# Hybrid attention encoder on one core: other homes for the second attention's first tiles, gates four deep, a fifth row buffer in the merge, another order of the first weights

## The chip, the core and the metric

The kernel runs on one NeuronCore of a Trainium2 chip. The metric is the device time of one execution in microseconds. The core's engines each work through their own instruction list in order: TensorE (PE: matmuls, and their weight loads as PEld), VectorE (DVE), ScalarE (ACT), GpSimd (POOL) and SyncE (SP), which here issues most DMAs; some are issued by ScalarE. An instruction waits for semaphores of others; what stands behind it on the same engine waits with it.

## The reference, cut to what matters

One layer of a bidirectional encoder over 2048 tokens of width 1024, all in float32:

```
h  = RMSNorm(x)
z  = h @ W_in  -> [q_A | k_A | v_A | q_B | k_B | v_B | gate_A | gate_B]
yA = windowed attention |t-s| <= 128, 8 heads, 2 groups of keys and values, ALiBi, a sink per head
yB = 2-D neighbourhood attention (8 heads, 32 rows x 64 columns, window 8 x 16) with a learned bias
x  = x + (sigmoid(gate_A) * (yA @ Wp_A) + sigmoid(gate_B) * (yB @ Wp_B)) @ W_out
x  = x + relu(RMSNorm(x) @ W_up)^2 @ W_down
out = RMSNorm(x)
```

## The kernel before, in words

Every float32 product is made of three matmuls on split operands: a high part (a cast to fp32r, by ScalarE) and a low part (the rest, by VectorE or GpSimd), so `mm3` (L200 to L203) issues high x high, high x low and low x high. Weights come as a slice of 128 columns in a tile `raw` (`load_slice`, L185 to L189; three buffers) and are split into `whl` (L176 to L178, two buffers): ScalarE casts (L177), GpSimd subtracts (L178).

The stages, in order:

1. The input projection of token blocks 0 and 1 in "quads" (matmuls at L252 to L254). Blocks 2 and 3 are only normalised and turned, and stored in DRAM (`h1d`).
2. The first attention (`attn_a`, from L667): 32 tiles (2 groups of 4 heads x 16 blocks of 128 queries). TensorE makes the scores (L680, L681; PSUM tag `s`, three banks); VectorE evicts them with bias and maximum (L682) into `sa`; ScalarE takes the exponent; GpSimd divides (L693). In a second step TensorE turns the probabilities (L699), they are split (`ph` L702, `pl` L703), TensorE multiplies them by the values (L704, L705, tag `av`, one bank), and the result goes by `ya` (L708, L709) to DRAM (`y_a`).
3. The second attention (`attn_b`, from L819): 32 units (8 heads `h`, each with four column blocks `j`). A unit loads queries `qb` (L824) and values `vb` (L827); per head `load_k` loads keys `kb0` or `kb1` (L814 to L816, 2.1 MB). Scores are L837, the eviction with bias L842 into `sb` (twelve buffers), the division L852 on GpSimd, the turning L864, the splits L869 and L870, the products L875; the result `yb` goes to `y_b`. `make_bias_b` adds the masks to a bias pattern `braw` on GpSimd (L805), into `biass` (j = 0 and 3, two buffers) or `biasl` (j = 1, kept for 2; one buffer).
4. The merge, four blocks of 512 tokens (from L1167). For each of eight features `f`, `gated(f, n)` (from L1174) multiplies weights by the pages of yA (n = 0) and yB (n = 1), 12 matmuls each; loads the stored gate `z` (L1183); takes its sigmoid (L1184, ScalarE); multiplies (L1185, VectorE). GpSimd adds both (L1197), ScalarE makes the high part `mh` (L1198), VectorE the low part `ml` (L1199). Then four rows of 128 tokens x two halves of 24 matmuls with W_out (PSUM `pt`, two banks), added to the row of x in `xr` by VectorE (L1217), normalised and turned (L1228). `load_y` (from L918) loads a block's yA and yB (`yraw`, L924) and splits them into pages (L930, L931).
5. The MLP: seven products for each quad (L252 to L254, `b`), up and down.

**Plain pieces.** What is left of the input projection, blocks 2 and 3, is cut into tiles of 24 matmuls (`qk_tile`, `v_tile`, `gate_tile`: L201 to L203 in PSUM tag `mm`) which `chain` (L714) yields in order, loading weights two tiles ahead and splitting them one ahead. `paced` (L736) sets each piece after the end of an attention unit: `at = n * 32 // total - lag`. In the first attention, 24 pieces; in the second, 44 with total = 40 and lag 4, of which pieces 20 to 43 are issued after `load_y(0)`. The pieces read the pages `hT` (blocks 2 and 3, L603 to L613), which are loaded (L609) and split ahead of everything else in stage 2.

**Who sets the order.** The program is written with waits (`issue_after`) and priorities by place; the order of each engine's list is then fixed when the program is built. It is the same in every execution.

**Homes.** On-chip memory is a stack from the left and one from the right. A new pool lies where an older one was closed, and a new tile waits until the tiles whose bytes it lies over are done. The first attention has, by the partition: on the right, from the end, `biasa0` (6 KB, bias of group 0), `va0` (8 KB), `ka0` (16 KB), `biasa1` (6 KB); on the left `ka1` (16), `va1` (8), `qa`, `sa`, `dist`, `ph`, `pl`, `ya`, `sta`. Group 0 is finished nine tiles before group 1. The second attention's pools of before, on the right: `masks` (12.5 KB), `braw` (2), `biass` (7.5), `biasl` (5), `kb0` (16), `qb` (6), `kb1` (16). So the masks lie over `biasa0` and `va0`; `braw`, `biass` and `biasl` over `va0` and `ka0`; `kb0` over the end of `ka0`, all of `biasa1` and free room; `qb` beyond it, where the left stack's last tiles (`ya`, `sta`) lie.

Of the kernel before, what the change touches and what calls it, by code (L numbers as in the profile page):

```python
# [8 lines left out]
F32 = mybir.dt.float32  # L9
# [6 lines left out]
D = 1024  # L16
# [6 lines left out]
P = 128  # L23
KC = D // P
NB = 4
BT = 512
# [66 lines left out]
def encoder_layer(ctx, tc, x, norm_mix, w_in, b_gate, sink, rpb, w_pa, w_pb, w_out,  # L93
# [12 lines left out]
    def pools(stack, side, tags, name):  # L106

        return {t: pool(f"{name}_{t}", side=side, stack=stack) for t in tags}
# [490 lines left out]
    ap_ = pools(s_a, "left", ("ka1", "va1", "qa", "sa", "dist", "ph", "pl", "ya", "sta"), "a")  # L599
    ap_.update(pools(s_a, "right", ("biasa0", "va0", "ka0", "biasa1"), "a"))  # L600
    hp = {}
    for b in (2, 3):
        hi, lo = [], []  # L603
        for p in range(2):
            h, l = (T(hpl[2 * (b - 2) + p], PAGE, F32R, "hT", 2) for _ in range(2))
            for n, (hh, ll) in enumerate(zip(halves(h), halves(l))):
                raw = T(wp, [P, KC, P], F32, "raw", 3).rearrange("p (k a) c -> p k (a c)", k=2)
                r = p * BT + n * 256
                SY.dma_start(raw, h1d[b - 2][r : r + 256, :].rearrange("(k p) t -> p k t", p=P))  # L609
                split(raw, hh, ll, V)  # L610
            hi.append(h)
            lo.append(l)
        hp[b] = hi, lo  # L613


    def qk_tile(col, scale, tiled=False):
# [96 lines left out]

    def chain(gens):  # L714

        for g in gens[:2]:
            next(g)
        next(gens[0])
        for k, g in enumerate(gens):
            if k + 2 < len(gens):  # L720
                next(gens[k + 2])
            if k + 1 < len(gens):
                next(gens[k + 1])
            yield from g
# [11 lines left out]
    def paced(filler, pieces, total, lag):  # L736

        for n in pieces:
            at = n * 32 // total - lag
            with tc.issue_after(done[at]) if at >= 0 else nullcontext():  # L740
                next(filler, None)

# [16 lines left out]
    for t in range(4):  # L759
        dense.append(qk_tile(O_KB + t * P, 0.125))  # L760
        dense.append(qk_tile(O_QB + t * P, 1.0, tiled=True))
        dense.append(v_tile(O_VB + t * P))
    fill = chain(dense + [gate_tile(f, (2, 3)) for f in range(16)])
    for g in (1, 0):
        make_bias_a(g)

# [13 lines left out]


    s_b = ExitStack()
    bp = pools(s_b, "right", ("masks", "braw", "biass", "biasl", "kb0", "qb", "kb1"), "b")
    bp.update(pools(s_b, "left", ("vb", "sb", "phb", "plb", "yb", "stb"), "b"))
    boff, bstart, btotal = bias_layout()
    masks = T(bp, [P, btotal], F32, "masks", 1)
    with tc.issue_after(began[20]):
# [28 lines left out]
        SY.dma_start(k[64:128, 1].bitcast(F32), kd[0:64])  # L816
        return k

    def attn_b(h, j, k, bias):  # L819
        e, t = h % 2, h // 2  # L820
        w, jt = B_W[j], JT[j]
        kp = 4 * w
        q = T(bp, [P, 4, P], F32R, "qb", 3)
        SY.dma_start(q.bitcast(F32), qs_b[t][e, :, j])  # L824
        yield
        v = T(bp, [P, 8, P], F32R, "vb", 3)
        SY.dma_start(v[: 4 * w].rearrange("p (b c) d -> p b (c d)", b=4).bitcast(F32),  # L827
                     vs_b[t][4 * B_C0[j] : 4 * (B_C0[j] + w), :, e * 256 : e * 256 + 256])
        st = T(bp, [P, 4, 4], F32, "stb", 6)
        mx, nm, sm, ri = (st[:, n, :] for n in range(4))  # L830
        kv = k.rearrange("p z (q f) -> p z q f", q=8)
        s = []
        for i in range(4):
            n = B_NR[i] * w
            ps = psum("s", 3)
            for z in range(2):
                PE.matmul(ps[:, :n], q[:, i, :],  # L837
                          kv[:, z, B_R0[i] // 4 : (B_R0[i] + B_NR[i]) // 4, 4 * B_C0[j] : 4 * (B_C0[j] + w)],
                          start=z == 0, stop=z == 1)
            o = boff[(jt, IT[i])]  # L840
            si = T(bp, [P, 512], F32, "sb", 12)
            V.tensor_tensor_reduce(out=si[:, :n], in0=ps[:, :n], in1=bias[:, o : o + n], scale=1.0, scalar=-3.0e38,  # L842
                                   op0=ALU.add, op1=ALU.max, accum_out=mx[:, i : i + 1])
            s.append(si)
        V.tensor_scalar(nm, mx, -0.125, None, ALU.mult)
        for i in range(4):
            n = B_NR[i] * w
            A.activation(s[i][:, :n], s[i][:, :n], AF.Exp, bias=nm[:, i : i + 1], scale=0.125, accum_out=sm[:, i : i + 1])
        V.reciprocal(ri, sm)
        for i in range(4):  # L850
            n = B_NR[i] * w
            G.tensor_scalar(s[i][:, :n], s[i][:, :n], ri[:, i : i + 1], 1.0, ALU.mult, ALU.mult)  # L852
        yield
        flush()
        po = psum("av", 1)
        first = True
        for pair in range(4):
            pt = psum("pt", 2)
            at, pieces = 0, []
            for c in (2 * pair, 2 * pair + 1):  # L860
                i0, ni = B_USE[c]
                for i in range(i0, i0 + ni):
                    rr = (4 * c - B_R0[i]) * w
                    PE.transpose(pt[:kp, at + (i - i0) * P : at + (i - i0 + 1) * P], s[i][:, rr : rr + kp], ident)  # L864
                pieces.append((c, i0, ni, at))
                at += ni * P
            ph = T(bp, [P, 512], F32R, "phb", 3)
            pl = T(bp, [P, 512], F32R, "plb", 3)
            A.copy(ph[:kp, :at], pt[:kp, :at])  # L869
            V.tensor_tensor(out=pl[:kp, :at], in0=pt[:kp, :at], in1=ph[:kp, :at].bitcast(F32), op=ALU.subtract)  # L870
            if pair == 0:
                pieces.reverse()
            for c, i0, ni, o in pieces:
                for z, src in enumerate((ph, pl)):
                    last = PE.matmul(po[:, i0 * P : (i0 + ni) * P], v[:kp, c, :],  # L875
                              src[:kp, o : o + ni * P], start=first, stop=(c == 7 and z == 1),
                              skip_group_check=True).ins
                    first = False
        done.append(last)

        y = T(bp, [64, BT], F32, "yb", 2)
        A.copy(y, po[64:128, :])
        V.tensor_tensor(out=y, in0=po[0:64, :], in1=y, op=ALU.add)
        put(y_b[t].rearrange("(e d) (i j t) -> e d i j t", e=2, i=4, j=4)[e, :, :, j, :],
            y.rearrange("d (i t) -> d i t", i=4))

    def all_b():
        for h in range(BH):
            k = load_k(h)
            for j in range(4):  # L890
                if j != 2:
                    bias = make_bias_b(h, JT[j])
                u = attn_b(h, j, k, bias)
                next(u)
                yield u

# [8 lines left out]

    units = ahead_of(all_b(), 1)
    drive((next(units) for _ in range(15)), live, False)
    paced(fill, range(20), 40, 4)
    flush()
    drive(units, live, True)  # L910
    flush()
# [23 lines left out]

    first_y = load_y(0)
    first_load = last_dma[0]
    paced(fill, range(20, 44), 40, 4)
    s_h.close()


# [6 lines left out]
    wo = []  # L948

    def load_wo(n):  # L950
        rv = T(p4x, [P, D], F32, "xr", 4)
        SY.dma_start(rv, w_out[0][n * P : (n + 1) * P, :])
        hl = T(pwo, [P, 2, D], F32R, "wo", 8)
        A.copy(hl[:, 0], rv)
        V.tensor_tensor(out=hl[:, 1], in0=rv, in1=hl[:, 0].bitcast(F32), op=ALU.subtract)
        wo.append(hl)
# [211 lines left out]
    for b in range(NB):  # L1168
        yh, yl = next_y
        mh = T(p4x, [P, KC, BT], F32R, "mh", 1)  # L1170
        ml = T(p4x, [P, KC, BT], F32R, "ml", 1)
        hls, gates = {}, {}

        def gated(f, n):  # L1174

            if n == 0:
                hls[f] = slice_of([(cols(w_pa[0], f * P), 4), (cols(w_pb[0], f * P), 4)])
            hl = hls[f]
            ps = psum("mm" if n == 0 else "s", 2 if n == 0 else 3)
            for c in range(4):  # L1180
                mm3(ps, hl[:, 0, 4 * n + c, :], hl[:, 1, 4 * n + c, :], yh[n][:, c], yl[n][:, c], c == 0, c == 3)
            g = T(wp, [P, 2, BT], F32, "z", 2)[:, 0] if n else T(p4, [P, BT], F32, "z", 4)
            SY.dma_start(g, zg[b][0][n, f * P : (f + 1) * P, :])  # L1183
            A.activation(g, g, AF.Sigmoid, bias=bg[:, 8 * n + f : 8 * n + f + 1])  # L1184
            V.tensor_tensor(out=g, in0=ps, in1=g, op=ALU.mult)  # L1185
            gates[f, n] = g
# [20 lines left out]
        tiles = []  # L1207
        for t in range(4):
            row0 = b * BT + t * P
            xt = load_tile(p4x, "xr", 4, xf[row0 : row0 + P])  # L1210
            for c in range(2):
                xc = xt[:, c * BT : (c + 1) * BT]
                ps = psum("pt", 2)
                for k in range(KC):
                    mm3(ps, mh[:, k, t * P : (t + 1) * P], ml[:, k, t * P : (t + 1) * P],
                        wo[k][:, 0, c * BT : (c + 1) * BT], wo[k][:, 1, c * BT : (c + 1) * BT], k == 0, k == KC - 1)
                V.tensor_tensor(out=xc, in0=ps, in1=xc, op=ALU.add)  # L1217
            flush()
            put(x2d[b][t * P : (t + 1) * P], xt)
            tiles.append(xt)  # L1220
# [227 lines left out]
```

## Time and profile before

| what | value |
| --- | --- |
| median of 3 runs | 2719.89 us (2717.86 to 2721.3) |
| the profiled execution's own time | 2720.12 us |
| its span, first to last instruction | 2718.3 us |
| mean granted TensorE clock | 0.990 |
| TensorE busy | 2637.6 us, 97% |
| stages, from the trace | first attention from 371.8 us, second from 689 us, merge from 1080 us, MLP from 1490 us |

How to read it: a line of a group or a timeline gives line number, engine, operation and tiles (out<-in). An idle time stands in brackets with the engine and line that ended it. In the rows of stretches the columns are the stretch, its length, then the busy time (and the number of instructions) of PE, PEld, DVE, ACT and POOL, the granted clock of TensorE, the share of DMA time and GB/s. A matmul's own length in the timeline (0.39 us) is more than the distance of two matmuls, since they are pipelined.

### The profile page before, as it was taken

The page shows a single profiled execution, that of the slowest core. Times are in us where ns is not written, and L with a number is a line of the kernel's source. Part 1 is how long each engine was busy: PE and PEld are TensorE (multiplying, and loading weights), DVE is VectorE, ACT ScalarE, POOL GpSimd, SP SyncE. Part 2 cuts the span into 40 slices and gives each one's busy share as a digit, 9 for nine tenths or more (in the row PEclk, how much of TensorE's full clock was granted, in tenths as well). Part 3 has the DMA queues.
Part 4 walks back from the last instruction along what each step waited for, and adds up shares of the span by engine and source line. Part 5 has one row for each costly group of instructions (what it writes and reads, how often), then busy time and mean ns, then how long its engine had stood idle before and what let it go on. Part 6 is the DMA issues. An engine that isn't in the chain of part 4 may idle for free.

```text
span 2718.3 us, 35079 instructions
## 1 busy us (share of the span) xinstructions
PE 2637.6 (97%) x12332; PEld 2184.2 (80%) x12332; DVE 1556.1 (57%) x2348; ACT 1251.4 (46%) x2229; POOL 843.8 (31%) x671
## 2 busy tenths in 40 slices
PE   7999999999899999898999999989999999999998
PEld 6888878777788888686787788878888888888887
DVE  7756466665454543633436667676664634545766
ACT  6334346665455555533533544554445333332444
POOL 1111233343555542531430456545553000000001
PEclk9999999999999999999999999999999999999999
DMA  4756385456777654734636556564435944445555
GB/s 148 200 155 196 135 240 149 109 142 162 210 198 189 184 152 141 260 121 151 229 109 225 190 200 209 178 208 163 144 129 190 335 155 159 149 149 178 174 191 169
DMA packets 329535, 480.86 MB, mean 177 GB/s; under 512 B 27896, under 2 KB 162168, under 8 KB 327184
## 3 DMA queue, kind: packets, MB, share of 16 engines
q1 hardware_dynamic: 300432, 445.06, 52.2%
q10 hardware_dynamic: 28928, 33.56, 3.9%
q8 instruction: 97, 1.59, 0.2%
q14 instruction: 78, 0.64, 0.1%
HBM read 323.28 MB, written 155.26 MB: 176 GB/s over the span
## 4 chain that ended last, share of the span: by engine, by line
PE 85%; DMA 6%; DVE 5%; ACT 2%; issue 1%; SPq 0%; POOL 0%; ACTq 0%; POOLq 0%; DVEq 0%
PE b L254 14%; PE b L252 14%; PE b L253 14%; PE mm L201 5%; PE mm L202 5%; PE mm L203 5%; PE zb L254 3%; PE zb L252 3%; PE zb L253 3%; PE av L875 2%; PE pt L201 2%; PE pt L202 2%; PE pt L203 2%; PE pt L864 2%; PE s L837 2%
## 5 line engine op out<-in xcount | busy, mean ns | idle before, releaser
L253 PE MATMUL b<-dwh,dah 128*128 128x512 f32 x896 | 348.5, 389 | 0.0
L254 PE MATMUL b<-dwh,dah 128*128 128x512 f32 x896 | 347.7, 389 | 0.0
L252 PE MATMUL b<-dwh,dah 128*128 128x512 f32 x896 | 338.1, 389 | 1.6 <-ACT dwh L248 1.6
L245 POOL TENSOR_TENSOR uc<-uc,uc 128x512 f32<-128x512 f32 x120 | 233.5, 1961 | 208.9 <-issue 136.3
L248 ACT CAST dah<-da 128x1024 fp32r<-128x1024 f32 (+1 forms) x128 | 121.0, 945 | 366.2 <-PE b L254 240.6
L249 DVE TENSOR_TENSOR dah<-da,dah 128x1024 fp32r<-128x1024 f32 (+1 forms) x128 | 139.3, 1090 | 224.4 <-ACT dah L248 219.6
L252 PE MATMUL b<-ubh,uwhlb 128*128 128x512 f32 x592 | 231.2, 391 | 3.3 <-DVE uc L245 2.2
L254 PE MATMUL b<-ubh,uwhlb 128*128 128x512 f32 x592 | 230.5, 391 | 3.2 <-DVE uwhlb L249 3.2
L253 PE MATMUL b<-ubh,uwhlb 128*128 128x512 f32 x592 | 230.9, 390 | 0.0
L201 PE MATMUL mm<-hT,whl 128*128 128x512 f32 x544 | 219.1, 403 | 4.5 <-ACT whl L177 2.3
L245 DVE TENSOR_TENSOR uc<-b,uc 128x512 f32<-128x512 f32 x160 | 108.8, 688 | 191.7 <-PE b L254 149.7
L203 PE MATMUL mm<-hT,whl 128*128 128x512 f32 x544 | 214.8, 395 | 0.0
L202 PE MATMUL mm<-hT,whl 128*128 128x512 f32 x544 | 214.5, 394 | 0.0
L178 POOL TENSOR_TENSOR whl<-raw,whl 128x1024 fp32r<-128x1024 f32 x66 | 160.2, 2428 | 148.8 <-ACT whl L177 142.4
L1338 POOL TENSOR_TENSOR st<-st,power 128x1 f32<-128x1 f32 x16 | 13.6, 857 | 613.8 <-DVE st L1337 613.6
L252 PEld LDWEIGHTS b<-dwh,dah 128*128 128x128 f32 x896 | 168.1, 188 | 36.9 <-ACT dwh L248 2.0
L254 PEld LDWEIGHTS b<-dwh,dah 128*128 128x128 f32 x896 | 168.2, 188 | 35.0
L253 PEld LDWEIGHTS b<-dwh,dah 128*128 128x128 f32 x896 | 168.2, 188 | 34.9
L252 PE MATMUL zb<-zh,zwhl 128*128 128x512 f32 x476 | 188.4, 398 | 3.8 <-DVE zh L464 2.6
L253 PE MATMUL zb<-zh,zwhl 128*128 128x512 f32 x476 | 188.0, 395 | 1.8 <-DVE zh L249 1.8
L254 PE MATMUL zb<-zh,zwhl 128*128 128x512 f32 x476 | 185.5, 395 | 0.4 <-DVE zwhl L249 0.3
L252 PEld LDWEIGHTS b<-ubh,uwhlb 128*128 128x128 f32 x592 | 111.7, 189 | 27.2 <-DVE uc L245 2.7
(243 smaller groups left out, 6236.5 us busy)
## 6 DMA issues: line engine op xcount, KB each, us to landing
at<-uc SPq DMA_DIRECT2D x224, 256.0 KB
da<-at SPq DMA_DIRECT2D x96, 512.0 KB
dw<-in_w_down_dram SPq DMA_DIRECT2D x160, 256.0 KB
uraw<-in_w_up_dram SPq DMA_DIRECT2D x32, 1024.0 KB
raw<-in_w_in_dram SPq DMA_DIRECT2D x34, 512.0 KB
zraw<-in_w_in_dram SPq DMA_DIRECT2D x16, 1024.0 KB
z<-zg SPq DMA_DIRECT2D x64, 256.0 KB
xin<-in_x_dram SPq DMA_DIRECT2D x16, 512.0 KB
```

Source lines behind the costliest of these rows:

```text
L178: G.tensor_tensor(out=hl[:, 1], in0=raw, in1=hl[:, 0].bitcast(F32), op=ALU.subtract)
L201: PE.matmul(ps, lh, rh, start=first, stop=False)
L202: PE.matmul(ps, lh, rl, start=False, stop=False)
L203: PE.matmul(ps, ll, rh, start=False, stop=last)
L245: return eng.tensor_tensor(out=out, in0=a, in1=b, op=op).ins
L248: A.copy(hi, src)
L249: eng.tensor_tensor(out=lo, in0=src, in1=hi.bitcast(F32), op=ALU.subtract)
L252: PE.matmul(ps, lh, rh, start=first, stop=False, skip_group_check=True)
L253: PE.matmul(ps, lh, rl, start=False, stop=False, skip_group_check=True)
L254: PE.matmul(ps, ll, rh, start=False, stop=last, skip_group_check=True)
L837: PE.matmul(ps[:, :n], q[:, i, :], kv[:, z, B_R0[i] // 4 : (B_R0[i] + B_NR[i]) // 4, 4 * B_C0[j] : 4 * (B_C0[j] + w)], start=z == 0, stop= ...
L864: PE.transpose(pt[:kp, at + (i - i0) * P : at + (i - i0 + 1) * P], s[i][:, rr : rr + kp], ident)
```

## The change

- **First weights.** The pages of block 2 are loaded, then the first plain tile's weights are loaded and split, then the pages of block 3, then the second tile's weights. Before, both blocks' pages stood ahead of all weights.
- **Homes.** Right pools of the second attention: `masks`, `qb`, `braw`, `biass`, `stb`, `kb0`, `biasl`, `kb1`. So `qb` lies over the end of `va0` and the start of `ka0`; `biasl` lies beyond `kb0`, over the left stack's last tiles. Left: `sb` becomes three pools of four (unit number modulo three), which lie first, over `ka1` (two) and `va1`; `vb` follows. `stb` has eight buffers for six. Head 0 takes its column blocks in the order 0, 3, 1, 2.
- **Plain pieces.** The second attention's `total` is 38 for 40 (the unit waited for is at most the last, 31).
- **Gates four deep.** For n = 1 one `z` tile of two halves serves two features, so its two buffers hold four gates.
- **Five rows.** `xr` has five buffers for four.

What is computed stays the same; only homes, buffers and order change.

```diff
-    for b in (2, 3):
+
+    def h_pages(b):
         hi, lo = [], []
...
         hp[b] = hi, lo
+
+    h_pages(2)
...
     def chain(gens):
-        for g in gens[:2]:
-            next(g)
-        next(gens[0])
...
-            at = n * 32 // total - lag
+            at = min(n * 32 // total - lag, 31)
...
-    fill = chain(dense + [gate_tile(f, (2, 3)) for f in range(16)])
+    dense += [gate_tile(f, (2, 3)) for f in range(16)]
+    next(dense[0])
+    next(dense[0])
+    h_pages(3)
+    next(dense[1])
+    fill = chain(dense)
...
-    bp = pools(s_b, "right", ("masks", "braw", "biass", "biasl", "kb0", "qb", "kb1"), "b")
-    bp.update(pools(s_b, "left", ("vb", "sb", "phb", "plb", "yb", "stb"), "b"))
+    bp = pools(s_b, "right", ("masks", "qb", "braw", "biass", "stb", "kb0", "biasl", "kb1"), "b")
+    bp.update(pools(s_b, "left", ("sb0", "sb1", "sb2", "vb", "phb", "plb", "yb"), "b"))
...
-        st = T(bp, [P, 4, 4], F32, "stb", 6)
+        st = T(bp, [P, 4, 4], F32, "stb", 8)
...
-            si = T(bp, [P, 512], F32, "sb", 12)
+            si = T(bp, [P, 512], F32, f"sb{n_u % 3}", 4)
...
-            for j in range(4):
+            for n, j in enumerate((0, 3, 1, 2) if h == 0 else range(4)):
...
-                u = attn_b(h, j, k, bias)
+                u = attn_b(4 * h + n, h, j, k, bias)
...
-    paced(fill, range(20), 40, 4)
+    paced(fill, range(20), 38, 4)
...
-    paced(fill, range(20, 44), 40, 4)
+    paced(fill, range(20, 44), 38, 4)
...
-        rv = T(p4x, [P, D], F32, "xr", 4)
+        rv = T(p4x, [P, D], F32, "xr", 5)
...
-            g = T(wp, [P, 2, BT], F32, "z", 2)[:, 0] if n else T(p4, [P, BT], F32, "z", 4)
+            if n == 0:
+                g = T(p4, [P, BT], F32, "z", 4)
+            else:
+                if f % 2 == 0:
+                    pair[0] = T(wp, [P, 2, BT], F32, "z", 2)
+                g = pair[0][:, f % 2]
...
-            xt = load_tile(p4x, "xr", 4, xf[row0 : row0 + P])
+            xt = load_tile(p4x, "xr", 5, xf[row0 : row0 + P])
```

More of the change, by code (lines that the diff above doesn't have):

```diff
@@ L817, in load_k, with attn_b @@
         return k
-    def attn_b(h, j, k, bias):
+    def attn_b(n_u, h, j, k, bias):
         e, t = h % 2, h // 2
@@ L1171, in encoder_layer @@
         ml = T(p4x, [P, KC, BT], F32R, "ml", 1)
-        hls, gates = {}, {}
+        hls, gates, pair = {}, {}, [None]
         def gated(f, n):
```

## The prediction

> **What bounds the kernel now.** I read the first part of the page, then who TensorE waits for, then the busy time of short stretches around each wait.
>
> ```profile
> PE 2637.6 (97%) x12332; PEld 2184.2 (80%) x12332; DVE 1556.1 (57%) x2348; ACT 1251.4 (46%) x2229; POOL 843.8 (31%) x671
> ```
>
> TensorE is busy 97% of the span, so an edit that removes no matmuls can give back only TensorE's idle time and what follows from it. The waits of TensorE, in total, times and longest:
>
> ```profile
> PE pt L201 <- DVE xr L1217: 6.3, 2, 5.7
> PE s L837 <- DMA qb<-qs_b: 6.0, 2, 3.7
> PE pt L203 <- DVE ml L1199: 4.3, 5, 1.1
> PE s L201 <- ACT page L930: 4.3, 1, 4.3
> PE mm L201 <- ACT whl L177: 2.9, 2, 2.3
> PE mm L201 <- DVE v L364: 2.2, 1, 2.2
> PE pt L201 <- ACT mh L1198: 1.8, 3, 1.3
> ```
>
> All seven lie between the last input quad and the MLP, where the diff works. Where they lie in time, and what they cost:
>
> ```profile
> 371.80:381.00 9.20, 5.97 (x24) 4.86 (x23) 5.63 (x18) 3.28 (x7) 4.70 (x2) 0.81 1.15 337
> 657.50:660.50 3.00, 0.80 (x5) 0.51 (x4) 0.99 (x2) 1.86 (x3) 0.00 (x0) 1.00 0.35 107
> 685.50:708.50 23.00, 14.88 (x64) 11.72 (x64) 10.84 (x39) 10.75 (x30) 12.43 (x16) 0.78 0.85 233
> 1088.00:1101.00 13.00, 7.50 (x23) 4.50 (x23) 5.98 (x5) 7.02 (x8) 5.42 (x3) 0.87 0.88 307
> 1143.50:1150.50 7.00, 4.96 (x15) 3.68 (x14) 5.35 (x6) 2.45 (x4) 1.79 (x1) 0.76 0.64 192
> 1231.50:1253.00 21.50, 12.40 (x44) 8.88 (x43) 7.42 (x9) 8.55 (x16) 5.21 (x4) 0.76 0.76 260
> 1336.50:1344.50 8.00, 5.66 (x21) 3.44 (x20) 5.35 (x6) 2.87 (x5) 4.14 (x3) 1.00 1.02 382
> 1351.00:1376.00 25.00, 25.00 (x113) 20.64 (x112) 7.37 (x13) 6.10 (x14) 1.09 (x2) 1.00 0.25 95
> ```
>
> The second number is the stretch, the third TensorE's busy time, the third from the end its granted clock. Idle is the difference: 3.2, 2.2, 8.1, 5.5, 2.0, 9.1 and 2.3 us. The last row is the undisturbed pace: 25.00 us for 113 matmuls, 0.22 us each, so a plain tile of 24 matmuls lasts 5.3 us. After most of these gaps the clock is halved:
>
> ```profile
> 374.90:378.90 4.00, 3.94 (x13) 3.62 (x14) 1.62 (x5) 1.05 (x2) 3.92 (x2) 0.57 1.12 361
> 689.40:692.90 3.50, 3.45 (x11) 3.13 (x12) 2.40 (x9) 0.00 (x0) 0.05 (x1) 0.51 1.04 368
> 702.20:706.60 4.40, 4.35 (x19) 4.24 (x19) 1.82 (x6) 0.58 (x1) 2.88 (x3) 0.51 0.27 87
> 1092.70:1095.70 3.00, 2.93 (x6) 1.78 (x6) 1.56 (x3) 1.58 (x2) 0.12 (x1) 0.51 1.02 410
> 1146.80:1150.30 3.50, 3.50 (x10) 2.75 (x9) 2.05 (x4) 1.01 (x2) 0.00 (x0) 0.51 0.63 174
> 1247.10:1252.70 5.60, 5.52 (x13) 4.36 (x14) 1.20 (x4) 2.47 (x6) 0.55 (x1) 0.51 0.99 352
> ```
>
> Length times the missing share: 1.7, 1.7, 2.2, 1.5, 1.7 and 2.7 us lost while busy. Idle plus clock, by place: start of the first attention 4.9; change to the second attention 2.2 + 8.1 + 3.9 = 14.2; change to the merge 7.0; merge block 0 to 1, 3.7; block 1, 11.8; block 2, 2.3. Together 43.9 us: the most that the change can return.
>
> The Trainium skill, page "TensorE: Matmul & The Clock Gate", Part 1 ("What's actually happening"), has the clock halve after at least one idle window of about 3.4 us. Here gaps of 2.0 to 2.3 us were followed by half clock too. By the rule the 1.7 us at 374.9 and at 689.4 would not come back with their gaps, and the sum would be 3 us smaller; I go by the rows.
>
> **The change, part by part.**
>
> *Order of first weights.* The first weight slice is now issued on SP ahead of block 3's pages, so that the first plain tile no longer waits for L177 (2.3 us). The slice takes one of three raw buffers; the third page of block 3 must then wait for its split on ACT and POOL. That still ends before the last quad (which ends at 371.8), so I see nothing late there. But in the changed order TensorE runs nearly three plain tiles first, and then tiles 3 to 5 of the attention with none between them. Those are VectorE's:
>
> ```profile
> L682 DVE CUSTOM_DVE_ANT_0 sa<-s,biasa,sink_t 128x384 f32<-128x384 f32 (+1 forms) x128 | 72.0, 596 | 36.8 <-PE pt L699 18.5 <-PE s L681 14.5 <-POOL sa L693 3.4
> L703 DVE TENSOR_TENSOR pl<-pt,ph 128x512 fp32r<-128x512 f32 x92 | 62.0, 683 | 18.8 <-ACT ph L702 18.3
> ```
>
> Four evictions (4 x 0.60) and three splits (3 x 0.68) are 4.4 us a tile before the small ones. TensorE's share without plain work is an estimated 3.3 us (six products of 512 columns at 0.22; 8 of 384 and 12 of 128 in proportion). Behind the evictions stand TensorE's next heads, which need one of three banks. I take 2 us of the 4.9; bounds -3 (three tiles each stalled 1 us, and a halved clock) and +4.9.
>
> *First tiles of the second attention.*
>
> ```profile
> 639.32 0.28 PE L681 MATMUL s<-ka,qa 128*128 128x256 f32 x1
> ```
> ```profile
> 641.01 0.57 SPq L814 DMA_DIRECT2D kb<-ks_b  x1
> 684.93 1.29 SPq L824 DMA_DIRECT2D qb<-qs_b  x3
> ```
> ```profile
> 648.05 0.40 PE L203 MATMUL mm<-hT,whl 128*128 128x512 f32 x1
> ```
> ```profile
> 644.00:646.00 2.00, 2.00 (x10) 1.65 (x9) 1.18 (x2) 0.34 (x1) 1.82 (x4) 1.00 0.99 325
> 646.00:648.00 2.00, 2.00 (x12) 1.70 (x11) 0.00 (x0) 0.40 (x1) 0.00 (x0) 1.00 1.07 354
> ```
>
> The keys (kb0) are asked for 1.7 us after the first attention's last score matmul, the queries (qb) 44 us later, when its last output tiles are gone: by size qb lies over them. After the change qb lies over group 0's keys and values and comes on SP ahead of kb0, and the score buffers lie over group 1's keys and values; so the scores may start as soon as kb0 is there. In the changed order the first one stands on TensorE right behind the matmul of 648.05. kb0 is 2.1 MB in three issues, now with only 0.8 MB of queries before it, long landed: at 325 to 354 GB/s that is 6.2 us after 642, plus a microsecond or two, 649 to 650. I price this new wait at 1 us (0 to 8.7, see the rivals). Behind it in TensorE's order stand the last weighted sums of the first attention. The third unit's bias (biasl) now lies over the last output tiles:
>
> ```profile
> 612.63 3.96 POOL L805 TENSOR_TENSOR biasl<-braw,masks 128x384 f32<-128x384 f32 x3 [3.45 <-DMA braw<-tab]
> ```
>
> It can begin when qb could before, at 685, and its first third is there 1.3 us later; TensorE has some 35 matmuls and transposes in between, so I take 1.5 us. What moved in front hides the rest: four plain tiles (21 us) are interleaved with the first two units instead of standing ahead of them. With the value tiles now asked for later than kb0, the DMA backlog that held the copy at L364 (2.2 us) is gone. 14.2 - 2.5, and 0.7 for small ones: 11 us (3 to 14).
>
> *Plain pieces spread* (38 for 40): in the changed order two whole tiles, 48 matmuls or 10.6 us, stand behind the last weighted sum of the second attention; before, none did. What they have to cover:
>
> ```profile
> 1083.33 0.28 PE L875 MATMUL av<-plb,vb 96*128 96x128 f32 x1
> ```
> ```profile
> 1088.45 0.34 SPq L924 DMA_DIRECT2D yraw<-y_b  x1
> ```
> ```profile
> 1092.03 0.62 ACT L930 CAST page<-yraw 128x512 fp32r<-128x512 f32 x1 [6.02 <-DMA yraw<-y_b]
> ```
>
> From the last sum to the split page are 9.3 us. 10.6 us of plain work and 2.6 of the first gate's own 12 matmuls cover that. What is late next is the weights of output (L954), which lie over the plain tiles' pages and wait for their end; they are wanted only after three gates. 6.5 of 7.0 us (3 to 7). The tiles come from the units before, whose engines have room (TensorE is the busy one there), so I cost that at nothing; uncovered it would be up to 3 us.
>
> *Gates four deep, five rows.*
>
> ```profile
> 1230.25 2.80 DVE L1199 TENSOR_TENSOR ml<-z,mh 128x512 fp32r<-128x512 f32 x1 [3.79 <-ACT mh L1198]
> 1238.14 2.51 DVE L1199 TENSOR_TENSOR ml<-z,mh 128x512 fp32r<-128x512 f32 x1 [3.89 <-ACT mh L1198]
> 1246.44 1.29 DVE L1217 TENSOR_TENSOR xr<-pt,xr 128x512 f32<-128x512 f32 x2 [5.79 <-DMA xr<-in_x_dram]
> ```
> ```profile
> 1235.93 0.72 ACT L1184 ACTIVATE z<-z,bg 128x512 f32<-128x512 f32 x1 [3.45 <-DMA z<-zg]
> 1237.49 0.61 ACT L1198 CAST mh<-z 128x512 fp32r<-128x512 f32 x1
> ```
> ```profile
> 1241.59 2.11 SPq L216 DMA_DIRECT2D xr<-in_x_dram  x4
> ```
>
> In block 1 the low parts follow each other by 7.9 us, where a gate's 24 matmuls take 5.3. ScalarE's sigmoid stands 3.45 us for its gate's load, and the copy to mh behind it, for which TensorE then waits (1.1 + 1.3 + 0.9 us). With four buffers the load is asked for two gates earlier; I take 2 of the 3.3. The row load is issued at 1241.59, when block 0's rows are free, and TensorE's 5.75 us end with it. A fifth buffer lets the first row of the next block be asked for a whole block earlier, and in SP's changed order it is; the next rows are wanted 10.6 us of matmuls later. So 5.75 + 2.7 + 2 = 10.5 us (8.5 to 11.8). Of 3.7 at blocks 0 to 1 I take 1.5 (0 to 3.7), of block 2's 2.3, 1 (0 to 2.3).
>
> **Sum.** 2 + 11 + 6.5 + 1.5 + 10.5 + 1 = 32.5 us. A new order of all queues always makes some waits: I deduct 3.5, two gaps of the size of the 1.7 us clock losses above. 29 us. The profiled execution took 2720.1 us (span 2718.3 and 1.8 around it), 0.2 over the median 2719.9: 2691.
>
> **Rivals.**
> 1. *The wait moves to kb0.* Its home still overlaps the bias of group 1, as before, and its issue cannot come earlier. If stores and weights share the transfer it lands not at 649 but near 655, and TensorE, with its queue in order, stands 7 us and a halved clock: 8.7 back, 2700. For: DMA share 1.0 in both rows above. Against: two loads of values, 0.9 MB, no longer stand before it.
> 2. *The merge keeps its pace*, since the weights' split on ScalarE and POOL rather than the gates' loads sets the 7.9 us, and the first attention's start costs 3: -3 + 8 + 3 + 0 + 8.5 + 0 - 3.5 = 13 us, 2707.
> 3. *It does not do what it says*: the waits come back elsewhere in the same size, because SP's one queue decides them: 2718. Against: the changed order has qb, the row and the gates ahead of what held them.
> 4. *Slower, by the gates' pairs.* A pair is free only when both its gates are added, and SP's queue stands behind its load, the weights too. In blocks 1 to 3 each of 24 gates has 48 matmuls (10.6 us) of its own and of the rows. If the cycle of a gate rose from 7.9 over 10.6, it would set the pace: at 12.0, 24 x 1.4 = 34 us, 2691 + 34 = 2725. Against: four buffers in pairs are never fewer than the two of before.
>
> **How the numbers follow.** Forecast 0.57, rival 1 0.20, rival 2 0.10, rival 3 0.06, rival 4 0.07. The predicted time is the forecast's. The bounds of its terms, mostly the first attention's start and the second's beginning, make 2681 to 2701; with rivals 1 and 2 and some of their spread, 2681 to 2711 leaves out less than 2 in 10. A measurement of this kernel can tell about 0.2% (5.4 us) from no change. Faster: 0.57 + 0.20 + 0.10 = 0.87; within 0.2%, 0.06; slower, 0.07.
>
> **What would show it.** Right: no wait of s for qb, one of at most 2 us for kb; no wait of s for the page (L930's line) and none of pt for xr near the second block; low parts under 7 us apart in block 1; the first attention's start shorter by about 2 us. Wrong: a gap with half clock ahead of the first score of the second attention, waits of s for the evictions in tiles 3 to 5 of the first, or DVE waiting for biasl.

## The result and the profile after

The changed kernel takes 2702.23 us (median of 6 runs, 2700.13 to 2706.06) against 2718.53 us (6 runs, 2714.09 to 2721.3) of the kernel before beside it: ratio 0.9944, 95% interval 0.9931 to 0.9956, that is 16.3 us less. The forecast was 29 less, with a range from 9 to 39 less. The profiled execution took 2706.06 us, its span is 2704.2.

Line numbers have moved by 3 to 12 (L680 is now L683, L837 is L842, L1199 is L1211, L1217 is L1229). Who TensorE waits for in the changed kernel, in total, times and longest (the largest, and the ones that the prediction named):

```profile
PE mm L350 <- ACT z L641: 7.0, 1, 7.0
PE pt L702 <- POOL sa L696: 5.3, 1, 5.3
PE pt L702 <- DVE pl L706: 4.1, 2, 3.6
PE pt L203 <- DVE ml L1211: 3.8, 5, 1.0
PE av L880 <- ACT phb L874: 2.6, 1, 2.6
PE s L842 <- DVE stb L847: 1.9, 3, 1.4
PE s L202 <- DVE page L937: 0.8, 1, 0.8
PE pt L201 <- DVE xr L1229: 0.6, 1, 0.6
PE s L842 <- DMA kb<-ks_b: 0.5, 1, 0.5
```

Six of the seven waits that the prediction listed are gone or small: for `xr` 0.6 us after 6.3, for `qb` none after 6.0, for the page 0.8 after 4.3, for the first weights (`whl` L177) none after 2.9, for `v` L364 none after 2.2, for `mh` 0.2 after 1.8. The low parts `ml` stay, 3.8 after 4.3. The two waits that were to take their place have the forecast size: the keys 0.5 us, the third unit's bias at most 1.4. VectorE itself stands much longer for that bias, which the prediction had named as a sign of being wrong; TensorE has other work for most of it:

```profile
DVE sb L847 <- POOL biasl L810: 6.8, 3, 6.1
```

What the list did not have before is its top: 7.0, 5.3 and 3.6 us in single pieces. Each is followed by half clock, as rows of stretches show (columns as in the prediction; each gap, then the stretch at half clock):

```profile
388.00:393.40 5.40, 0.10 (x2) 0.05 (x1) 1.91 (x7) 3.15 (x10) 2.56 (x6) 0.77 1.03 313
390.90:397.70 6.80, 4.35 (x12) 3.48 (x13) 0.00 (x0) 1.48 (x7) 5.94 (x9) 0.50 0.61 232
444.40:448.20 3.80, 0.16 (x2) 0.09 (x2) 1.45 (x4) 3.21 (x11) 0.45 (x1) 1.00 0.88 236
448.90:452.40 3.50, 2.98 (x8) 2.69 (x9) 3.50 (x10) 0.85 (x2) 2.00 (x4) 0.51 0.19 37
761.30:768.40 7.10, 0.13 (x2) 0.09 (x2) 0.80 (x4) 0.73 (x2) 0.19 (x1) 0.86 1.00 243
766.40:773.20 6.80, 4.89 (x19) 4.51 (x19) 2.17 (x4) 4.39 (x12) 3.03 (x3) 0.50 0.89 249
```

**The gap at 393 us.** GpSimd's timeline in the changed kernel:

```profile
376.59 2.18 POOL L655 TENSOR_SCALAR biasa<-dist 128x384 f32<-128x384 f32 x4
390.68 2.04 POOL L655 TENSOR_SCALAR biasa<-dist 128x384 f32<-128x384 f32 x4 [11.91 <-DMA zg<-zc]
392.81 1.85 POOL L696 TENSOR_SCALAR sa<-sa,sta 128x256 f32<-128x256 f32 x4
```

and in the kernel before:

```profile
383.01 1.85 POOL L693 TENSOR_SCALAR sa<-sa,sta 128x256 f32<-128x256 f32 x4 [3.33 <-DVE sta L691]
384.82 2.05 POOL L652 TENSOR_SCALAR biasa<-dist 128x384 f32<-128x384 f32 x4
```

GpSimd builds the distance bias of both groups. In the changed order group 0's stands ahead of the first tile's scaling; it waits 11.91 us for the tile whose bytes it lies over to be stored (`zg`), and the scaling, and with it TensorE's first transpose, waits behind it. Group 0 is not wanted before the eighth tile. Before, it stood behind the first scaling.

**The gap at 768 us**, in the middle of the second attention, at a plain tile that the diff does not touch. SP's and ScalarE's timelines:

```profile
750.33 1.88 SPq L629 DMA_DIRECT2D qs_b<-z  x3
...
753.10 0.60 SPq L819 DMA_DIRECT2D kb<-ks_b  x1
753.75 0.49 SPq L820 DMA_DIRECT2D kb<-ks_b  x1
755.20 0.49 SPq L821 DMA_DIRECT2D kb<-ks_b  x1
755.74 0.60 SPq L629 DMA_DIRECT2D qs_b<-z  x1
```
```profile
766.90 0.57 ACTq L174 DMA_DIRECT2D y_b<-yb  x1
767.67 0.59 ACT L641 COPY z<-mm 128x512 f32<-128x512 f32 x1 [11.79 <-DMA vb<-vs_b]
```

A plain tile of queries leaves its `z` by four stores; three go out, then come the 2 MB of the fourth head's keys, and only then the fourth store. ScalarE stands 11.79 us, first for the store of `y_b`, then at the copy into the same `z`; TensorE's L350 needs that copy. The timeline names the load of `vb`, which was issued behind the keys too. Which of the two ScalarE instructions counts, it does not tell.

### The profile page after: what moved, and what is told of

Its sections match the earlier page's. It is cut to its first block, busy times and chain, and to the rows that moved or that the text cites. A ratio compares the mean times of both kernels' runs of the same rounds, so it can differ in the third digit from the quotient of the medians.

```text
span 2704.2 us, 35025 instructions
## 1 busy us (share of the span) xinstructions
PE 2629.0 (97%) x12332; PEld 2177.3 (81%) x12332; DVE 1558.3 (58%) x2348; ACT 1255.8 (46%) x2231; POOL 839.4 (31%) x671
## 4 chain that ended last, share of the span: by engine, by line
PE 82%; DVE 6%; DMA 6%; ACT 3%; issue 2%; POOL 1%; SPq 0%; ACTq 0%; POOLq 0%; DVEq 0%
PE b L252 15%; PE b L253 15%; PE b L254 15%; PE mm L203 5%; PE mm L201 5%; PE mm L202 5%; PE zb L254 3%; PE zb L252 3%; PE zb L253 3%; PE av L880 2%; PE s L842 2%; PE pt L869 2%; DMA z<-zg 2%; PE pt L203 2%; PE pt L201 2%
```

## The experiments

A ratio is that of a kernel to the kernel before, measured beside it on the same chip, with its 95% interval; 0.001 is 2.7 us. The kernel before took 2718.5 us beside the changed kernel, and 2720.8 to 2723.3 beside the others, so kernels are compared by ratios and not by their times; two ratios can be told apart from about 0.002 on. "Beyond full pace" is worked out from the trace: the time from each matmul's start to the next one's, less what the same shape takes in the fastest tenth, summed over a stretch; it holds the waits and the half clock. Its sum falls from 238.3 to 224.2 us with the change, 14.1, which is the difference of the two spans. By stretches put together from ones of 50 us:

| us beyond full pace | 350-450 | 650-750 | 750-800 | 1000-1050 | 1050-1150 | 1200-1250 | 1300-1400 |
| --- | --- | --- | --- | --- | --- | --- | --- |
| before | 17.5 | 26.0 | 8.3 | 9.6 | 17.0 | 14.5 | 7.2 |
| after | 22.8 | 15.1 | 15.1 | 11.4 | 6.9 | 4.2 | 10.1 |
| bias_late | 20.4 | 16.3 | 14.6 | 10.4 | 6.3 | 4.2 | 8.7 |
| no_weights | 18.0 | 13.8 | 16.5 | 11.0 | 5.6 | 6.2 | 10.5 |
| no_attn | 19.6 | 28.5 | 9.1 | 8.3 | 6.0 | 4.2 | 8.6 |
| no_merge | 21.3 | 16.8 | 16.2 | 12.5 | 8.8 | 10.9 | 7.6 |
| keys_later | 24.5 | 15.1 | 7.8 | 11.4 | 5.4 | 6.2 | 11.3 |
| no_spread | 22.6 | 16.5 | 14.6 | 10.3 | 16.5 | 5.1 | 8.6 |
| no_pair | 22.2 | 17.2 | 16.0 | 12.0 | 9.7 | 3.5 | 6.5 |
| weights_keys | 18.1 | 14.4 | 8.5 | 11.5 | 3.4 | 4.2 | 9.3 |
| spread_rows | 18.1 | 28.3 | 9.0 | 8.6 | 8.6 | 3.4 | 7.4 |
| store_sp | 22.3 | 15.3 | 18.5 | 12.0 | 6.6 | 4.6 | 8.3 |
| bias_keys | 18.8 | 14.3 | 9.4 | 11.3 | 5.0 | 3.7 | 8.9 |
| wk_no_pair | 18.0 | 17.0 | 8.2 | 12.8 | 6.7 | 2.8 | 6.4 |

Each row is one execution. How far executions differ can be seen in the first column: seven of the kernels (after, no_attn, no_merge, keys_later, no_spread, no_pair, store_sp) have the same order of the four compute engines up to 600 us, and read 19.6 to 24.5, 22.2 on average. The profiled execution of the changed kernel was the slowest of its six (3.8 us over the median), that of no_attn the fastest of its six (6.6 us under). Stretches are by time, so they hold slightly other work in a kernel that is ahead or behind.

My theory was that the places on the list gave back what was forecast, and that two new waits took it away again; the rival, that the engines around TensorE bind there anyway, so that a wait removed is a wait moved.

**Group 0's bias later.**

```diff
-    for g in (1, 0):
-        make_bias_a(g)
+    make_bias_a(1)
...
+                if (g, i) == (1, 2):
+                    with tc.issue_after(scaled[1]):
+                        make_bias_a(0)
```

> The changed kernel with one thing moved: the four GpSimd operations that build the bias of group 0 (L655) stand behind the scaling of the second tile of the first attention instead of ahead of that of the first; the order on the other four engines is the changed kernel's. Theory A: in the changed kernel GpSimd stood 11.91 us in that build, waiting for a store of zg, with the first tile's scaling behind it, and this is the whole of TensorE's 5.3 us ahead of the first transpose (L702) and of the 6.83 us at half clock there. Then the wait falls under 1 us, no half clock stands at the start of the first attention, and the time is 2702.2 - 5.3 - 3.4 = 2693.5 us (2692 to 2696), 0.991 of before. Rival B: the first tiles are bound by VectorE's evictions and the weights' splits, whatever GpSimd does; another wait of 3 to 5 us takes the place, and the time is 2699 to 2703.

Measured: 2699.68 us, ratio 0.9923 (0.9911 to 0.9935). The wait for GpSimd is gone, as theory A has it, but only half of the time came. Now TensorE stands for the queries:

```profile
PE s L683 <- DMA qa<-qs_a: 2.9, 2, 1.9
```

Half clock begins at 405.4 us instead of 390.9. Beyond full pace, 350 to 400 us falls by 4.7 us, and 400 to 450 rises by 2.3. The first is outside what executions of the same order read there (5.2 to 10.1 us; here 4.3), the second is not far outside (13.8 to 15.3; here 16.1). So A's cause is right for the first gap, and B is right on part of the size.

**The old order of the first weights.**

```diff
-    def h_pages(b):
+    for b in (2, 3):
...
-    h_pages(2)
...
+        for g in gens[:2]:
+            next(g)
+        next(gens[0])
...
-    next(dense[0])
-    next(dense[0])
-    h_pages(3)
-    next(dense[1])
```

> The changed kernel with the order of the first weights undone: all hidden pages first, then the first slices, as before. Theory A (the new order cost time, since it put the two builds of the bias together on GpSimd ahead of the first scaling): between 350 and 450 us TensorE's time beyond full pace falls from 22.8 to the 17.6 us of before, and the time is about 2702.2 - 5 = 2697 us (2695 to 2699). Rival B (the forecast: the new order gains 2 us): 2704 us, and without any effect 2702.

Measured: 2699.85 us, 0.9924 (0.9910 to 0.9937); 18.0 us beyond full pace at the start, the 17.5 of before again. The new order costs 0.0020, 5.4 us; it does not gain. The two intervals overlap a little; the traces bear it out, since all five kernels with the old order read 17.5 to 18.1 at the start, and the seven with the new one 19.6 to 24.5.

**The second attention as before.** Pools, one ring of `sb`, six of `stb`, units 0 1 2 3:

```diff
-    bp = pools(s_b, "right", ("masks", "qb", "braw", "biass", "stb", "kb0", "biasl", "kb1"), "b")
-    bp.update(pools(s_b, "left", ("sb0", "sb1", "sb2", "vb", "phb", "plb", "yb"), "b"))
+    bp = pools(s_b, "right", ("masks", "braw", "biass", "biasl", "kb0", "qb", "kb1"), "b")
+    bp.update(pools(s_b, "left", ("vb", "sb", "phb", "plb", "yb", "stb"), "b"))
```

> The changed kernel with the second attention's part undone: its pools, its one ring of twelve score tiles, six statistics tiles and the order 0 1 2 3 of the first head's units, as before. If the forecast of 11 us for that part holds and the new wait of 7.0 us (z L641, with its half clock about 10 us) was made elsewhere: 2702.2 + 11 = 2713 us (2711 to 2716), with that wait still there. If the new wait comes with that part's order of loads: the wait is gone, and what the part gained and lost nearly cancels: 2701 to 2705 us.

Measured: 2705.3 us, 0.9942 (0.9927 to 0.9956), the changed kernel's 0.9944 within the intervals. The wait for the queries is back and the one for `z` nearly gone:

```profile
PE s L842 <- DMA qb<-qs_b: 5.9, 2, 3.3
PE mm L350 <- ACT z L641: 0.7, 1, 0.7
```

The second branch holds: this part gained what was forecast (650 to 750 us: 28.5 against 15.1) and made the 7.0 us wait. With its order of loads undone, all four stores of that `z` stand ahead of the keys:

```profile
748.80 2.53 SPq L629 DMA_DIRECT2D qs_b<-z  x4
...
758.88 0.42 SPq L819 DMA_DIRECT2D kb<-ks_b  x1
```

**The merge as before** (`xr` four, each late gate in its own tile).

> The changed kernel with the merge's two parts undone (four row tiles in place of five, each late gate in a tile of its own). If the forecast holds (6.5 + 1.5 + 10.5 + 1 = 19.5 us from these two): 2702 + 19.5 = 2721.7 us (2716 to 2724), with the waits of pt for xr and of the clock in block 1 back. Rival: the waits in the merge went because the plain tiles are spread otherwise and the earlier work ends sooner; then undoing this costs under 5 us, 2702 to 2707.

Measured: 2709.27 us, 0.9964 (0.9951 to 0.9976): 0.0020 lost, not 0.007. The wait for the row is back,

```profile
PE pt L201 <- DVE xr L1223: 7.0, 2, 6.4
```

but the change to the merge stays short (1050 to 1100 us: 4.2 us, before 12.0). The forecast in this expectation put the spread's share to these two parts; that was my slip, not the prediction's.

**The fourth head's keys later.** Only SP's order changes:

```diff
-            k = load_k(h)
+            with tc.issue_after(loaded[-4]) if h == 3 else nullcontext():
+                k = load_k(h)
```

> The changed kernel with the three loads of the fourth head's keys (kb, 2 MB) issued behind the values' load of the unit before the last three, that is, behind the fourth store of the plain tile ahead of the one that waited; the order on the other four engines is the changed kernel's. Theory C+D (the 7.0 us of L350 for z L641 come from the 2 MB of keys that stand in SP's queue ahead of what ScalarE waits for): the gap and the 6.83 us at half clock at 766 us go, and the time is 2702.2 - 7.0 - 3.4 = 2692 us (2690 to 2696). Rival E: the wait moves to the next plain tile, whose three last stores now stand behind the keys, or to the keys' first use; 2699 to 2703 us.

Measured: 2698.21 us, 0.9906 (0.9890 to 0.9922), 10 us less than the changed kernel by the ratios, 7.8 by the traces; the time itself lies 2 us above the range that was expected, against a kernel before that took 2722.0 us here. TensorE's list has no L350 any more; 750 to 800 us is at 7.8 us beyond full pace, as before the change. Three stores of the next tile now stand behind the keys; TensorE has no wait for them, so rival E falls. SP's order in this kernel:

```profile
751.32 0.65 SPq L629 DMA_DIRECT2D qs_b<-z  x1
...
755.63 0.61 SPq L821 DMA_DIRECT2D kb<-ks_b  x1
...
757.76 2.01 SPq L629 DMA_DIRECT2D qs_b<-z  x3
```

**The stores of y_b from SP.**

```diff
-        flush()
+        flush(eng=SY)
```

> The changed kernel with the stores of y_b in the second attention issued from SP's queue instead of ScalarE's. Theory C: the 7.0 us wait comes from the store of y_b that stands ahead of the copy to z on ScalarE and waits for an earlier transfer; then the wait goes, and the time is about 2692 us. Theory D: the copy itself waits for the fourth store out of the tile that it overwrites, which stands behind the 2 MB of keys; then the wait stays at 5 to 7 us, and the time at 2700 to 2704 us.

Measured: 2705.61 us, 0.9942 (0.9927 to 0.9957). TensorE's wait and what ScalarE waits for around it:

```profile
PE mm L350 <- ACT z L641: 9.9, 1, 9.9
```
```profile
ACT z L641 <- DMA qs_b<-z: 12.9, 1, 12.9
```

Theory C falls, D holds: with no store on ScalarE the copy still stands, and now the trace names the stores out of `z` themselves. That it is the fourth store, behind the keys, and not one of the first three, is shown by the run with the keys later.

**The old spread** (`total` 40).

> The changed kernel with the plain pieces paced over 40 units' worth again, as before. If the spread is what shortened the change from the second attention to the merge (1050 to 1100 us: 12.0 us beyond full pace before, 5.4 after, 4.2 with the merge's parts undone): 6 us slower, 2708 us (2706 to 2710), with the waits of L201 to L203 at the start of the merge back. If that came from the second attention's order or from the gates: no difference, 2701 to 2704 us. The wait for z L641 stays either way, since the loads around it keep their order.

Measured: 2712.6 us, 0.9965 (0.9954 to 0.9976). The wait at the start of the merge is back:

```profile
PE s L201 <- ACT page L936: 5.9, 1, 5.9
```

1050 to 1150 us is at 16.5 us beyond full pace again (after 6.9). The spread shortened the change to the merge, as the prediction had it.

**Each late gate in its own tile**, five rows kept.

> The changed kernel with five row tiles, but each late gate of the merge in a tile of its own again (two deep in place of four). With both parts undone the kernel lost 2709.3/2720.8 against 2702.2/2718.5, some 5 us. If the row tiles hold all of that (the wait of L201 for xr, 6.4 us): 2701 to 2704 us, and block 1 has no wait of more than 2 us. If the gates hold it: 2706 to 2709 us, with the low parts of block 1 late again.

Measured: 2702.71 us, 0.9929 (0.9915 to 0.9944). The row tiles hold the gain; the pairs give nothing that can be told. The table shows what stands against what: with pairs 1050 to 1150 us is shorter by 2.8 us (6.9 for 9.7) and 1300 to 1400 longer by 3.6 (10.1 for 6.5).

**Both repairs, old weights' order and later keys.**

> The changed kernel without the new order of the first weights and with the fourth head's keys loaded later: both repairs together. If the two waits are independent, the ratios add up: 0.9944 - (0.9944 - 0.9924) - (0.9944 - 0.9906) = 0.9886 of before, about 2689 us against 2720 (2686 to 2692). If the one only shifts the other's place: 0.990 to 0.992.

Measured: 2688.61 us, 0.9876 (0.9858 to 0.9894). The ratios add up within the interval, so the two waits are independent. No kernel of the study is faster (the two others that have both repairs lie within its interval); 0.0124 of 2720 us is 34 us less than before, where the change gave 16.

**Both repairs, the new weights' order kept and the bias later.**

> The changed kernel with the order of the first weights kept, group 0's bias built behind the second tile's scaling, and the fourth head's keys loaded later. If the waits are independent: 0.9944 - (0.9944 - 0.9923) - (0.9944 - 0.9906) = 0.9885, the same as without the order of the weights. If that order gains the 2 us of the forecast once GpSimd doesn't hold it: 0.9877.

Measured: 2690.87 us, 0.9882 (0.9864 to 0.9900). Freed from GpSimd's build, the new order of the weights is worth nothing that these intervals can tell.

**The spread and the fifth row alone**, on the kernel before.

> The kernel before with two of the parts alone: the pieces paced over 38 and the fifth row tile. By the terms as measured so far (spread 12.99 - 5.39 = 7.6 us of TensorE between 1050 and 1100 us, row tiles 10.87 - 4.15 = 6.7 us between 1200 and 1250 us, and their half clock in it): 2720 - 14 = 2706 us, ratio 0.9948 (0.993 to 0.996). If the second attention's part and the weights' order give nothing on top in the changed kernel, this alone is as fast as it (0.9944).

Measured: 2700.59 us, 0.9912 (0.9898 to 0.9926): 24 us, more than the whole change and more than the 14 expected. The profiled executions differ by 19 (238.3 to 219.3 us beyond full pace), all of it between 1050 and 1250 us. Most of the other 5 is the kernel before, whose median beside this one was 2723.3 us where its profiled execution took 2720.1.

**Both repairs, without the pairs.**

> The version with both repairs (old order of the first weights, keys later), with the late gates of the merge each in a tile of its own again. It parts two terms: against the version with both repairs it gives the gates' pairs, against the spread and the fifth row tile alone (0.9912) it gives the second attention's part. If the pairs are worth the 2.9 us that the traces show between 1050 and 1150 us (9.74 beyond full pace without them, 6.89 with them): 0.9876 + 0.0011 = 0.9887. If they give nothing: 0.9876. If they cost what the changed kernel with and without them differ by (0.9944 and 0.9929): 0.986. The second attention's part: its forecast of 11 us makes 0.9912 - 0.0040 = 0.987.

Measured: 2689.16 us, 0.9881 (0.9865 to 0.9898). The pairs give nothing here either: by the same sums 1100 to 1150 us costs 4.0 us without them and 1.0 with, 1300 to 1400 us 6.4 and 9.3. Against the spread and the row alone the second attention's part gives 0.9912 - 0.9881 = 0.0031, 8.4 us; the two intervals just touch.

## Why the prediction was right in direction and 13 us too far

The measured 2702 us lie in the stated range of 2681 to 2711, but just outside the forecast's own bounds of 2681 to 2701. That part of the range was there for rivals 1 and 2. Rival 1 did not happen, and of rival 2 only the loss at the first attention's start and the pace of the low parts did. So the direction was foreseen for the right reasons, but that the time lies in the range is in part luck.

- **What bounds the kernel.** Right. All that moved are TensorE's waits and the half clock behind them.
- **Order of first weights, +2 us.** Wrong, and the step is the sentence that nothing is late there. The order costs 5.4 us (no_weights), below the lower bound of -3; the trace has 17.5 to 22.8. The gain itself came: from 350 to 375 us the time beyond full pace falls from 3.0 to 0.1 us, and the wait for L177 is gone. Two losses outweigh it. I followed the third page and its splits on ScalarE and GpSimd, but not GpSimd's own list, where the bias of group 0 moved ahead of the first scaling: from 375 to 400 us the seven kernels of one order read 7.5 us on average, those with the old order 4.6, those with the bias later 4.2 and 4.8. And 400 to 450 us costs 13.8 to 15.3 us in the seven and 13.9 and 16.1 with the bias later, but 10.0 to 10.4 in the five with the old order. There TensorE stands 3.6 us at 448 us in every kernel with the new order; with the old order its longest wait between 400 and 450 us is 1.8. So by the traces the bias is the smaller of the two losses. By the ratios moving it gives back as much as undoing the order (0.9923 and 0.9924), so the second loss is seen in the traces alone; what makes it is open (below). The evictions that I feared cost 3.0 us in seven pieces of at most 0.5, no more than before (3.5).
- **First tiles of the second attention, 11 us.** Right as far as the prediction looked: 26.0 to 15.1, 10.9 us. Keys 0.5 us for 1, third bias 1.4 for 1.5. Rival 1 did not happen. But the part gave back 6.7 us at 768 us, and perhaps the 1.8 between 1000 and 1050 us; without the first of these it is worth 8.4 us.
- **Spread, 6.5 us.** Right in mechanism: between 1050 and 1150 us it gives 16.5 - 6.9 = 9.6 us, where the prediction had 6.5 + 1.5 = 8.0 with block 0 to 1. That the tiles come from the units before at no cost holds: nothing shows between 800 and 1000 us.
- **Fifth row.** Right: 6.4 us of wait come back without it. The 10.5 us of block 1 came too (14.5 to 4.2), but the row alone brings them (spread_rows and no_pair read 3.4 and 3.5), so that the 2 us of the gates in that sum are luck.
- **Gates four deep, 2 of 3.3 us.** Wrong. The low parts were to follow each other in under 7 us. They do not, in block 1 of the changed kernel:

```profile
1212.61 1.48 DVE L1211 TENSOR_TENSOR ml<-z,mh 128x512 fp32r<-128x512 f32 x1 [2.78 <-ACT mh L1210]
1220.52 2.52 DVE L1211 TENSOR_TENSOR ml<-z,mh 128x512 fp32r<-128x512 f32 x1 [2.98 <-ACT mh L1210]
1227.98 2.53 DVE L1211 TENSOR_TENSOR ml<-z,mh 128x512 fp32r<-128x512 f32 x1 [3.74 <-ACT mh L1210]
```

  They stand 7.9 and 7.5 us apart, as before (the pair before these is 6.2 apart). What rival 2 said of the merge's pace holds, without its price: the pace did not bind TensorE once the row came early (3.5 us beyond full pace without pairs).
- **Deduction of 3.5 us for new waits.** The mis-sized term. 750 to 800 us costs 6.7 us more, 1000 to 1050 us 1.8 more: 8.5 us. Rival 3 gave the mechanism (SP's one queue decides) with too high a price.
- **The sum.** -5.3 + 10.9 + 10.1 + 10.3 - 2.9 (1300 to 1400 us) = 23.1, less 8.5, is 14.6 us; the spans differ by 14.1. The forecast's 32.5 - 3.5 fails by 7.3 at the first weights, 5.0 at the deduction, and 3.9 at blocks 2 and 3. Its 2691 us is the time that the change takes without its two new waits (2688.6 and 2690.9), but with other terms: there the order of the weights gives nothing, the gates nothing, and the spread more.
- **The price of the clock.** Right to go by the rows: in the kernel with both repairs the clock is lost after a gap of 2.56 us (last section).

What stays open: the 3.6 us of L702 for `pl` at 448 us, which went with the order of the first weights but was never taken away alone, and the 1.8 us between 1000 and 1050 us. There ScalarE's sigmoids of the first gates stand among the last units of the attention, and TensorE waits behind them:

```profile
1034.07 1.28 ACT L1196 ACT_TABLE_LOAD   x1
1038.07 1.28 ACT L853 ACT_TABLE_LOAD   x1
1041.73 1.28 ACT L1196 ACT_TABLE_LOAD   x1
```
```profile
1037.12 0.38 PE L880 MATMUL av<-phb,vb 96*128 96x256 f32 x1 [2.56 <-ACT phb L874]
```

There are three loads of the function table, where before, no_attn and spread_rows have one. The gap is gone with the second attention's part undone (8.3 us between 1000 and 1050), but also with the spread undone: no_spread has three loads too, at 1042.6 to 1051.1 us, and no wait for `phb` over 0.4 us there. So the loads alone do not make it; that it is the sigmoids was not tried by itself.

## What to carry to other kernels

Follow each engine's whole list past the moved step, not only the engines whose tile moves: a small build for later use, placed ahead of the first tile's work, cost here what the reordering gained (2.9 us each by the traces). When several short stores free a buffer, look for a large load that falls between them in the queue: three of four stores out early is as late as none. Undo each part by itself before keeping it; two of the five parts carried 24 us, one gave 8 after a repair, and two nothing or less.

## What the runs showed of the hardware

**The half clock keeps to a grid.** In each of the fourteen profiles all starts of half clock lie on one grid of 3.413 us, to 0.003 of its step, and between 200 and 2600 us it lasts 3.41, 6.83, 10.24 or 13.65 us. The Trainium skill, page "TensorE: Matmul & The Clock Gate", Part 1 ("What's actually happening"), has such a window of 3413 ns that runs freely; the traces agree. They differ on how much of it must be idle: between 200 and 2600 us, 72 of 72 grid steps at full clock in which TensorE idled over 1.88 us were followed by half clock, 11 of 32 with 1.6 to 1.88, and 3 of 374 with 0.4 to 1.6. About half a step is enough, by idle times that rest on the modelled ends of the matmuls. So one and the same gap of 2.56 us (L880 for `phb`) costs nothing more in the changed kernel, where the grid cuts it in two:

```profile
1032.61:1036.02 3.41, 1.95 (x17) 1.71 (x16) 2.30 (x5) 3.38 (x5) 1.88 (x1) 1.00 0.88 308
1036.02:1039.44 3.42, 2.12 (x12) 1.79 (x13) 1.60 (x3) 3.39 (x7) 0.47 (x1) 1.00 0.31 98
```

and a stretch at half clock in the kernel with both repairs, where it lies in one step:

```profile
1016.88:1020.29 3.41, 0.83 (x5) 0.63 (x6) 2.39 (x3) 3.38 (x7) 1.75 (x1) 1.00 0.52 188
1020.29:1023.70 3.41, 3.41 (x13) 2.82 (x12) 0.49 (x1) 3.40 (x9) 0.00 (x0) 0.50 0.62 168
```

**A short VectorE operation behind a GpSimd one.** In the changed kernel an operation on 4 elements takes 2.12 us, and ends with GpSimd's split:

```profile
442.75 2.12 DVE L688 TENSOR_SCALAR sta<-sta 128x4 f32<-128x4 f32 x1
```
```profile
442.47 2.37 POOL L178 TENSOR_TENSOR whl<-raw,whl 128x1024 fp32r<-128x1024 f32 x1 [4.32 <-ACT whl L177]
```

At 389.59 us the same operation takes 0.17:

```profile
389.59 0.17 DVE L688 TENSOR_SCALAR sta<-sta 128x4 f32<-128x4 f32 x1
```

The Trainium skill, page "SBUF — State Buffer", section "Who interferes with whom", has GpSimd and certain VectorE operations share a pair of ports that the first one holds to its end; these rows agree. It is not one case: of the 64 such operations in the two attentions of the changed kernel (L688 and L850) 19 take over 0.5 us, up to 2.3; each of the 19 begins while GpSimd is in an operation and ends 0.02 to 0.03 us after it. The exponents of that tile wait for this operation, ahead of the 3.6 us gap at 448 us; that the gap comes from it is read from the trace, not tried. In the kernel before, the same operation of the same tile takes 2.08 us too, and TensorE then waits 1.8 us, so this alone does not explain the longer gap.
